# Two attentions' scores: two heads per pass on the two row halves of the array, and retention's first pair of heads moved into its value projection

## The chip, the core and the metric

The kernel runs on one core of a Trainium2 chip. TensorE (PE in the profile) multiplies matrices: it loads 128 stationary columns (a weight load, PEld in the profile), streams up to 512 moving columns past them and adds the products into PSUM. VectorE (DVE), ScalarE (ACT) and GpSimd (POOL) work element by element; SyncE (SP) issues DMAs. The metric is the device time of one execution in microseconds (us); lower is better.

## The reference, cut to what matters

The reference is a two-layer encoder trunk on x of shape (1, 512, 1024), all in float32. Each layer mixes the sequence with two mixers side by side and then runs a convolutional feed-forward part. The change touches one mixer of each layer: the dilated attention of layer 0 and the retention of layer 1.

```python
# dilated attention: 8 heads of 64; three windows, each a softmax with its own log-sum-exp
q, k = rope(q.reshape(shp)), rope(k.reshape(shp))
...
s = jnp.einsum('bdhnqe,bdhnke->bdhnqk', qb, kb) * E ** -0.5
...
# retention: 4 heads, keys of 64, values of 128, a decay per head in both directions
q = rope(q) * RET_KEY_DIM ** -0.5
k = rope(k)
...
scores = jnp.einsum('bhnid,bhnjd->bhnij', q, k) * dmat[:, None]
o = jnp.einsum('bhnij,bhnje->bhnie', scores, v)
```

The kernel computes both with the full 512 x 512 scores of a head. In dilated attention the three windows become one softmax, with the log of how many windows hold a key added to its score (the table `lnc`). In retention the chunked recurrence becomes a product of q and k, times a table of decays (`gen`), times v.

## The kernel before, in words

**Number format.** A float32 matrix is split into a high part in the format fp32r (`hi`) and the rest (`lo = x - hi`). A product a*b is then three products, hi*hi, hi*lo and lo*hi, added in PSUM (`mm3`, L262 to L265). Weights are split on arrival: ACT makes `whi`, DVE makes `wlo` (`fetch`, L240). There are four buffers each of `whi` and `wlo` (WB = 4) and three of the raw weights. `get` keeps one further weight tile ready beside the one it hands out.

**PSUM.** Two groups of four banks: `acc` (sums that live long, and the transposes `tp` of dilated attention) and `wk` (short ones; the scores `sp` of dilated attention and `rsp` of retention are here). Each bank holds 128 x 512 float32.

**Rotary and the scores.** A tile of q or k holds two heads of 64 rows each, one above the other, for all 512 positions. `rope_in` (L448) copies it out of PSUM and swaps its 32-row blocks by DMA. `rope_out` (L461) rotates it and splits it in a stacked form: one operand has, for head e, `hi` on the head's own 64 rows and `lo` on the other 64; the other operand (`moving`) has `hi` on both halves (the second by a POOL copy) and, in a second pair of columns, `lo` on the head's rows and zeros (a POOL memset) on the rest. So the three products of a head are two matrix products over all 128 rows (`mm_stack`, L483): hi*hi and lo*hi at once, then hi*lo.

**Dilated attention** (L500). After the projections of two pairs of heads and of v, a loop goes over 16 units (4 pairs of heads x 4 blocks of 128 queries). Step u issues the scores of unit u (two heads, two products each), DVE's add and minimum, ACT's exponential and POOL's scaling; the transposes (`tp`, 8 of them) of unit u-2, copied to `pT` by ACT and DVE; and the products with v (`op`) of unit u-3. Projections of the later pairs (`dqk`) stand between. In `op` the two heads lie side by side: each uses 64 of the array's 128 columns.

**Retention** (L1033). Four projections (`first`, `rqk`) give q and k; `proj_tok` (L293) makes v from four chunks of weights, 24 products each, into four banks `pt`; ACT copies them to `rv`. Then come the decay tables `gen`, the scores of head 0, and a loop over heads: the scores of head h+1, then the 16 products `ro` of head h with v. For each score tile DVE multiplies by `gen` into `sd`, which frees the `wk` bank.

**Order.** Each engine executes its own instructions strictly in the order in which they stand in its queue, and waits for others by semaphores. That order is not the one of the source: a scheduler places each instruction by its own estimate of when its operands are ready. An instruction that waits holds all that stand behind it on its engine.

Of the kernel before, what the change touches and what calls it, by code (L numbers as in the profile page):

```python
# [11 lines left out]
ALU = mybir.AluOpType  # L12
# [150 lines left out]
class K:  # L163
# [129 lines left out]
    def proj_tok(self, n, out_fn, filler=None):  # L293

        accs = [self.acc(nm=f"pt{t}") for t in range(NT)]
        for c in range(4):
            w = self.get()
            for t in range(NT):
                for j in range(2):
                    kk = 2 * c + j  # L300
                    self.mm3(accs[t], n.ht(kk, slice(t * 128, t * 128 + 128)), (w[0][:, j, :], w[1][:, j, :]), kk == 0, kk == KT - 1)
# [159 lines left out]
    def rope_out(self, pool, rope, t, sw, moving, tag, bufs):  # L461

# [37 lines left out]
    def dilated(self, n, tail):  # L500
        nc, I = self.nc, self.I
        V = nc.vector
        with ExitStack() as ctx:
# [7 lines left out]
            def project(p, what, ps=None):  # L511
# [3 lines left out]
                qk[p, what] = self.rope_out(dp, rope, *self.rope_in(dp, ps)[:2], what == "k", "d" + what, 3)  # L515
# [40 lines left out]
            for i in range(4):  # L556
# [3 lines left out]
                if i < 2:  # L560
                    qk[0, "qk"[i]] = self.rope_out(dp, rope, *rin[i][:2], i == 1, "d" + "qk"[i], 3)
            with self.tc.issue_after(rin[3][2].ins):
                for i in (2, 3):
                    qk[1, "qk"[i % 2]] = self.rope_out(dp, rope, *rin[i][:2], i == 3, "d" + "qk"[i % 2], 3)
# [468 lines left out]
    def retention(self, n, order):  # L1033
        nc, I = self.nc, self.I
        V = nc.vector
        with ExitStack() as ctx:
# [8 lines left out]
            def rot(i):  # L1045
                which, s = i // 2, i % 2
                qk[which, s] = self.rope_out(rp, rope, *rin[i][:2], which == 0, f"r{which}{s}", 1)
# [12 lines left out]
            self.proj_tok(n, lambda t, a: nc.scalar.copy(v[:, t, :], a))  # L1060
# [5 lines left out]
            for h in range(4):  # L1066
# [339 lines left out]
```

## Time and profile before

| | |
|---|---|
| time, median of 3 runs | 1319.92 us (1319.66 to 1320.06) |
| the profiled execution's own time | 1319.69 us |
| its span, first to last instruction | 1317.9 us |
| PE busy / DVE / ACT / POOL, share of the span | 99% / 57% / 40% / 11% |
| chain that ended last | PE 87%, DVE 7%, ACT 2% |
| granted TensorE clock over the span | 0.999 of full speed |

A timeline row gives an instruction's start and how long it took. On PE the second is not its cost in a stream: matrix products overlap, and the cost of one is the distance to the start of the next. A product of 512 columns takes 0.39 us from start to end, but the next one starts 0.227 us after it. Rows with xN merge N like instructions in a row; their time runs from the first start to the last end. Idle time and what ended it stand in square brackets.

### The profile page before, as it was taken

Reading aid. Unit: us, or ns where it says so; the run is one execution under the profiler, and the core shown is the slowest. Engines: PE = TensorE matmul, PEld = TensorE weight load, DVE = VectorE, ACT = ScalarE, POOL = GpSimd, SP = SyncE. Lnnn points to the kernel's source line nnn. Section 1 sums busy time; section 2 is a strip of 40 time slices with the busy share of each in tenths; the row PEclk is TensorE's granted clock in tenths of the full one; section 3 lists DMA queues with packets and bytes.
Section 4 is the critical chain, followed back from the end, with each engine's and each line's share of the span. In section 5 each row is a group of like instructions: output and inputs, shape, how many; then the busy total and the mean of one; then the engine's idle time right before and its main releaser. Section 6 shows DMA issues by size and latency. Waiting matters only on the chain.

```text
span 1317.9 us, 17629 instructions
## 1 busy us (share of the span) xinstructions
PE 1302.9 (99%) x6977; PEld 1092.6 (83%) x6977; DVE 750.7 (57%) x1089; ACT 526.9 (40%) x837; POOL 144.4 (11%) x175
## 2 busy tenths in 40 slices
PE   8999999999999999999999999999999999999997
PEld 7877888888988888888889887888888888888886
DVE  5777659977744432444437828879754443344432
ACT  5466548235433321333326334532433331133332
POOL 2454120013000000000002200024100000000001
PEclk9999999999999999999999999999999999999999
DMA  7430113411333332333323513330343333233321
GB/s 227 127 103 25 52 33 112 130 49 61 119 101 99 98 96 81 112 96 96 96 80 112 163 41 100 93 96 19 90 122 99 99 99 96 81 113 96 96 80 64
DMA packets 161025, 123.61 MB, mean 94 GB/s; under 512 B 6985, under 2 KB 134477, under 8 KB 160944
## 3 DMA queue, kind: packets, MB, share of 16 engines
q1 hardware_dynamic: 160798, 122.43, 31.6%
q8 instruction: 55, 0.90, 0.3%
q14 instruction: 26, 0.21, 0.1%
q10 hardware_dynamic: 146, 0.07, 0.0%
HBM read 117.23 MB, written 2.10 MB: 91 GB/s over the span
## 4 chain that ended last, share of the span: by engine, by line
PE 87%; DVE 7%; ACT 2%; DMA 1%; issue 1%; SPq 1%; POOL 1%; POOLq 0%; ACTq 0%; DVEq 0%
PE gup L264 11%; PE gup L265 11%; PE gup L263 11%; PE oacc L264 7%; PE oacc L265 7%; PE oacc L263 7%; PE pt L263 2%; PE pt L264 2%; PE pt L265 2%; PE first L264 2%; PE first L265 2%; PE first L263 2%; PE ap L263 1%; PE ap L264 1%; PE ap L265 1%; PE hap L263 1%
## 5 line engine op out<-in xcount | busy, mean ns | idle before, releaser
L252 DVE TENSOR_TENSOR wlo<-raw,whi 128x1024 fp32r<-128x1024 f32 x192 | 236.2, 1232 | 305.0 <-ACT whi L251 300.3
L251 ACT CAST whi<-raw 128x1024 fp32r<-128x1024 f32 (+1 forms) x197 | 206.1, 1047 | 424.7 <-PE gup L264 183.7
L263 PE MATMUL gup<-hh,whi 128*128 128x512 f32 x656 | 255.2, 389 | 0.0
L264 PE MATMUL gup<-hl,whi 128*128 128x512 f32 x656 | 255.2, 389 | 0.0
L265 PE MATMUL gup<-hh,wlo 128*128 128x512 f32 x656 | 255.2, 389 | 0.0
L263 PEld LDWEIGHTS gup<-hh,whi 128*128 128x128 f32 x656 | 123.2, 188 | 25.6
L264 PEld LDWEIGHTS gup<-hl,whi 128*128 128x128 f32 x656 | 123.2, 188 | 25.4
L265 PEld LDWEIGHTS gup<-hh,wlo 128*128 128x128 f32 x656 | 123.2, 188 | 25.4
L263 PE MATMUL oacc<-whi,ghi 128*128 128x512 f32 x352 | 137.1, 389 | 0.0
L265 PE MATMUL oacc<-whi,glo 128*128 128x512 f32 x352 | 137.0, 389 | 0.0
L264 PE MATMUL oacc<-wlo,ghi 128*128 128x512 f32 x352 | 136.9, 389 | 0.0
L265 PEld LDWEIGHTS oacc<-whi,glo 128*128 128x128 f32 x352 | 66.1, 188 | 13.7
L263 PEld LDWEIGHTS oacc<-whi,ghi 128*128 128x128 f32 x352 | 66.1, 188 | 13.7
L264 PEld LDWEIGHTS oacc<-wlo,ghi 128*128 128x128 f32 x352 | 66.1, 188 | 13.6
L428 DVE TENSOR_TENSOR sl<-gup,sl 128x512 f32<-128x512 f32 x42 | 29.0, 692 | 81.1 <-PE gup L265 81.1
L313 DVE TENSOR_TENSOR x<-oacc,x 128x512 f32<-128x512 f32 x64 | 43.2, 684 | 48.6 <-PE oacc L265 48.6
L427 ACT ACTIVATE sl<-c 128x512 f32<-128x512 f32 x44 | 27.8, 632 | 89.2 <-DVE c L365 89.2
L263 PE MATMUL first<-hh,whi 128*128 128x256 f32 x192 | 54.9, 288 | 0.0
L264 PE MATMUL first<-hl,whi 128*128 128x256 f32 x192 | 54.4, 284 | 0.2 <-DVE hl L224 0.2
L265 PE MATMUL first<-hh,wlo 128*128 128x256 f32 x192 | 54.2, 283 | 0.0
L104 POOL TENSOR_SCALAR ss<-ss 128x1 f32<-128x1 f32 x16 | 5.0, 311 | 429.3 <-ACT jk L102 429.3
L263 PE MATMUL pt<-whi,hh 128*128 128x512 f32 x128 | 50.1, 391 | 0.1
(422 smaller groups left out, 2336.4 us busy)
## 6 DMA issues: line engine op xcount, KB each, us to landing
raw<-in_ffn_w_in_dram SPq DMA_DIRECT2D x88, 512.0 KB, 3.8
raw<-in_ffn_w_out_dram SPq DMA_DIRECT2D x44, 512.0 KB, 3.7
raw<-in_ab_w_in_dram SPq DMA_DIRECT2D x28, 512.0 KB, 3.9
raw<-in_cd_w_in_dram SPq DMA_DIRECT2D x24, 512.0 KB, 4.6
x<-in_x_dram SPq DMA_DIRECT2D x16, 256.0 KB, 4.2
raw<-in_ab_w_out_dram SPq DMA_DIRECT2D x8, 512.0 KB
raw<-in_cd_w_out_dram SPq DMA_DIRECT2D x8, 512.0 KB, 3.6
rs<-rt SPq DMA_DIRECT2D x32, 64.0 KB, 2.0
```

The source lines that it names most:

```text
L104: nc.gpsimd.tensor_scalar(ss[:, 1:2], ss[:, 0:1], s, EPS, op0=ALU.add, op1=ALU.add)
L251: self.nc.scalar.copy(hi, raw)
L252: (self.nc.gpsimd if self.pool_lo else self.nc.vector).tensor_tensor(lo, raw, hi, op=ALU.subtract)
L263: mm(out, a[0], b[0], start=start, stop=False)
L264: mm(out, a[0], b[1], start=False, stop=False)
L265: return mm(out, a[1], b[0], start=False, stop=stop)
L313: self.nc.vector.tensor_add(xs, acc, xs)
L427: nc.scalar.activation(sl, c, AF.Silu)
L428: nc.vector.tensor_mul(sl, up, sl)
```

## The change

The operands of both score products are now split plainly, `hi` and `lo` of all 128 rows. The scores of the two heads of a pair are made together by `mm_pair`: six products, head 0 on rows 0 to 63 and head 1 on rows 64 to 127 of the array, three each, in turn, each head into its own PSUM bank. The POOL copies and memsets of `rope_out` go, and its ACT and DVE work is one instruction each where there were two. In retention the tables `gen` are made pair by pair inside `scores`; the scores of the first pair are issued in the value projection ahead of its chunk 3 (RS = 3), those of the second behind the products `ro` of head 0; the `sd` tiles have three buffers where there were two.

```diff
-    def proj_tok(self, n, out_fn, filler=None):
+    def proj_tok(self, n, out_fn, within={}):
...
         for c in range(4):
+            within.get(c, lambda: None)()
             w = self.get()
...
-        o = pool.tile([128, 4 if moving else 2, S], F32R, tag=tag, name=tag, bufs=bufs)
-        half = [slice(0, 64), slice(64, 128)]
-        for e in range(2):
-            a, b = half[e], half[1 - e]
-            nc.scalar.copy(o[a, e], t[a])
-            nc.vector.tensor_sub(o[a, 2 + e] if moving else o[b, e], t[a], o[a, e])
-            if moving:
-                nc.gpsimd.memset(o[b, 2 + e].bitcast(F32), 0.0)
-                nc.gpsimd.tensor_copy(o[b, e], o[a, e])
+        o = pool.tile([128, 2, S], F32R, tag=tag, name=tag, bufs=bufs)
+        self.split(o[:, 0], o[:, 1], t)
         return o
...
-    def mm_stack(self, out, a, b, e, cols):
-        self.nc.tensor.matmul(out, a[:, e, cols], b[:, e], start=True, stop=False)
-        self.nc.tensor.matmul(out, a[:, e, cols], b[:, 2 + e], start=False, stop=True)
+    def mm_pair(self, outs, a, b, cols):
+
+        for x, y in ((0, 0), (0, 1), (1, 0)):
+            for e in range(2):
+                r = slice(64 * e, 64 * e + 64)
+                self.nc.tensor.matmul(outs[e], a[r, x, cols], b[r, y], start=x + y == 0, stop=x == 1)
...
-                for e in range(2):
-                    sp = self.wk(nm="sp")
-                    self.mm_stack(sp, qk[p, "q"], qk[p, "k"], e, slice(i * 128, i * 128 + 128))
+                sps = [self.wk(nm="sp") for _ in range(2)]
+                self.mm_pair(sps, qk[p, "q"], qk[p, "k"], slice(i * 128, i * 128 + 128))
+                for e, sp in enumerate(sps):
...
-            self.proj_tok(n, lambda t, a: nc.scalar.copy(v[:, t, :], a))
...
-            def scores(h):
-                q, k = qk[0, h // 2], qk[1, h // 2]
+            def scores(s):
+                for h in (2 * s, 2 * s + 1):
+                    nc.scalar.activation(gen[:, h, :], rel[0], AF.Copy, scale=ld[:, h:h + 1])
+                    V.scalar_tensor_tensor(gen[:, h, :], rel[1], ld[:, 4 + h:5 + h], gen[:, h, :], op0=ALU.mult, op1=ALU.add)
+                    nc.scalar.activation(gen[:, h, :], gen[:, h, :], AF.Exp)
                 for j in range(4):
-                    sp = self.wk(nm="rsp")
-                    self.mm_stack(sp, k, q, h % 2, slice(j * 128, j * 128 + 128))
-                    t = rp.tile([128, S], F32, tag=f"sd{j}", name=f"sd{j}", bufs=2)
+                    sps = [self.wk(nm="rsp") for _ in range(2)]
+                    self.mm_pair(sps, qk[1, s], qk[0, s], slice(j * 128, j * 128 + 128))
...
-            scores(0)
+            self.proj_tok(n, lambda t, a: nc.scalar.copy(v[:, t, :], a), {RS: lambda: scores(0)})
...
             for h in range(4):
-                if h < 3:
-                    scores(h + 1)
...
+                if h == 0:
+                    scores(1)
...
+RS = 3
```

What this does to the order on an engine is shown at three places. PE in the last unit of dilated attention, before (`sp` are the scores, `tp` the transposes, `op` the products with v; numbers tell the banks apart):

```order
L546 MATMUL op_1233<-pT_1308,dv_196 64x128
L484 MATMUL sp_1359<-dk_1086,dq_923 128x512
L485 MATMUL sp_1359<-dk_1086,dq_923 128x512
L484 MATMUL sp_1365<-dk_1086,dq_923 128x512
L485 MATMUL sp_1365<-dk_1086,dq_923 128x512
L535 MATMUL tp_1374<-ident_76,smx_1284 128x128 x4
```

and now:

```order
L542 MATMUL op_1225<-pT_1304,dv_196 64x128
L481 MATMUL sp_1357<-dk_1078,dq_911 128x512
L481 MATMUL sp_1358<-dk_1078,dq_911 128x512
L481 MATMUL sp_1357<-dk_1078,dq_911 128x512
L481 MATMUL sp_1358<-dk_1078,dq_911 128x512
L481 MATMUL sp_1357<-dk_1078,dq_911 128x512
L481 MATMUL sp_1358<-dk_1078,dq_911 128x512
L531 MATMUL tp_1374<-ident_76,smx_1283 128x128 x4
```

The unit keeps its place between `op` and `tp`; its four products are six, and the two banks take turns.

PE at the start of the value projection's chunk 3 in retention, now (`pt` are the projection's banks, `rsp` the score tiles; before, 24 products `pt` stand here and all `rsp` come after them):

```order
L265 MATMUL pt3_6252<-whi_6285,hl1_5867 128x512
L481 MATMUL rsp_6349<-r00_6171,r10_6232 128x512
...
L481 MATMUL rsp_6362<-r00_6171,r10_6232 128x512
L263 MATMUL pt0_6249<-whi_6315,hh1_5865 128x512
L264 MATMUL pt0_6249<-wlo_6316,hh1_5865 128x512
L481 MATMUL rsp_6373<-r00_6171,r10_6232 128x512 x3
L481 MATMUL rsp_6374<-r00_6171,r10_6232 128x512 x3
L481 MATMUL rsp_6385<-r00_6171,r10_6232 128x512 x3
L481 MATMUL rsp_6386<-r00_6171,r10_6232 128x512 x3
L265 MATMUL pt0_6249<-whi_6315,hl1_5867 128x512
```

Twelve products fill the four `wk` banks, two of the projection follow, then twelve more into the same banks, here three of one head and then three of the other; the other 22 of chunk 3 stand behind them.

DVE at the same place (`r11` is the last rotated tile, `wlo` a weight tile's low part, `sd` the scores times the decays), before:

```order
L473 TENSOR_TENSOR r11_6252<-room_6223,r11_6252 64x512 x2
L252 TENSOR_TENSOR wlo_6568<-raw_6565,whi_6567 128x1024
L252 TENSOR_TENSOR wlo_6598<-raw_6595,whi_6597 128x1024
L1079 TENSOR_TENSOR sd0_6408<-rsp_6405,gen_5980 128x512
L1079 TENSOR_TENSOR sd1_6413<-rsp_6410,gen_5980 128x512
```

and now:

```order
L224 TENSOR_TENSOR r11_6238<-room_6217,r11_6238 128x512
L252 TENSOR_TENSOR wlo_6568<-raw_6565,whi_6567 128x1024
L252 TENSOR_TENSOR wlo_6598<-raw_6595,whi_6597 128x1024
L1075 TENSOR_TENSOR sd0_6357<-rsp_6349,gen_5980 128x512
L1075 TENSOR_TENSOR sd0_6359<-rsp_6350,gen_5980 128x512
```

On DVE nothing has moved: the two `wlo` still stand ahead of the first `sd`, whose scores PE now makes a chunk earlier.

DVE early in dilated attention, units 1 to 3, before (`smx<-sp` reads the scores; `dq` is the low part of the rotated q of pair 2, `pT` the copy of a transpose):

```order
L537 COPY pT<-tp 128x512
L527 RECIPROCAL st<-st 128x2
L466 TENSOR_TENSOR rt<-rt,rope 128x512
L467 TENSOR_TENSOR rt<-rt,rs 128x512
L524 ISA smx,st<-sp,lnc 128x512
...
L473 TENSOR_TENSOR dq<-rt,dq 64x512 x2
L252 TENSOR_TENSOR wlo<-raw,whi 128x1024
L527 RECIPROCAL st<-st 128x2
L537 COPY pT<-tp 128x512
```

and now:

```order
L533 COPY pT<-tp 128x512
L523 RECIPROCAL st<-st 128x2
L466 TENSOR_TENSOR rt<-rt,rope 128x512
L467 TENSOR_TENSOR rt<-rt,rs 128x512
L224 TENSOR_TENSOR dq<-rt,dq 128x512
L252 TENSOR_TENSOR wlo<-raw,whi 128x1024
L520 ISA smx,st<-sp,lnc 128x512
...
L533 COPY pT<-tp 128x512
```

Here `dq` and `wlo` have moved ahead of the two reads of unit 3's scores (`...` stands for the second one and its flag).

## Rows read from the trace of the kernel before

**Rows 1.** The page: the span, the busiest engines, and the chain of waits by engine.

```profile
span 1317.9 us, 17629 instructions
...
PE 1302.9 (99%) x6977; PEld 1092.6 (83%) x6977; DVE 750.7 (57%) x1089; ACT 526.9 (40%) x837; POOL 144.4 (11%) x175
...
PE 87%; DVE 7%; ACT 2%; DMA 1%; issue 1%; SPq 1%; POOL 1%; POOLq 0%; ACTq 0%; DVEq 0%
```

**Rows 2.** The waits of PE over the whole span, longest in total first: what waited, for whom, us in total, times, longest.

```profile
PE nrowp L91 <- DMA nrow<-in_norm_mix_dram: 3.8, 1, 3.8
PE nt L152 <- DVE xn L139: 0.8, 1, 0.8
PE tp L535 <- ACT pT L537: 0.7, 1, 0.7
```

**Rows 3.** The timeline of PE in dilated attention: one unit and the start of the next (start, time, engine, line, operation, tiles, shapes, count).

```profile
118.16 0.50 PE L484 MATMUL sp<-dk,dq 128*128 128x512 f32 x1
118.49 0.40 PE L485 MATMUL sp<-dk,dq 128*128 128x512 f32 x1
118.73 0.40 PE L484 MATMUL sp<-dk,dq 128*128 128x512 f32 x1
118.96 0.39 PE L485 MATMUL sp<-dk,dq 128*128 128x512 f32 x1
119.19 1.03 PE L535 MATMUL tp<-ident,smx 128*128 128x128 f32 x8
120.16 1.09 PE L546 MATMUL op<-pT,dv 128*64 128x128 f32 x16
121.18 0.50 PE L484 MATMUL sp<-dk,dq 128*128 128x512 f32 x1
```

**Rows 4.** The same timeline where transposes follow `op` directly, at the end of dilated attention.

```profile
130.26 1.09 PE L535 MATMUL tp<-ident,smx 128*128 128x128 f32 x8
```

**Rows 5.** The timeline of PE in the gated delta part of layer 0: transposes `vp` of 64 x 64 blocks, the first four of the x12 on rows 0 to 63, the next four on rows 64 to 127, the rest on rows 0 to 63 again, all into output rows 0 to 63; the x4 all on one half. Between them, products over the whole array.

```profile
269.35 0.63 PE L917 MATMUL vp<-ident,P 64*64 64x64 f32 x12 [0.20 <-DVE P L903]
269.92 0.50 PE L263 MATMUL oacc<-whi,yh 128*128 128x512 f32 x1
270.35 0.41 PE L917 MATMUL vp<-ident,P 64*64 64x64 f32 x4
270.69 0.50 PE L264 MATMUL oacc<-wlo,yh 128*128 128x512 f32 x1
271.02 0.39 PE L265 MATMUL oacc<-whi,yl 128*128 128x512 f32 x1
271.25 0.39 PE L263 MATMUL oacc<-whi,yh 128*128 128x512 f32 x1
```

**Rows 6.** The timeline early in dilated attention, rows of DVE, ACT and PE where PE waits.

```profile
76.33 0.69 DVE L467 TENSOR_TENSOR rt<-rt,rs 128x512 f32<-128x512 f32 x1 [1.86 <-POOL rs L465]
...
77.55 0.69 DVE L524 CUSTOM_DVE_ANT_0 smx<-sp,lnc 128x512 f32<-128x512 f32 x1
...
79.71 1.23 DVE L252 TENSOR_TENSOR wlo<-raw,whi 128x1024 fp32r<-128x1024 f32 x1
...
80.93 0.67 DVE L537 COPY pT<-tp 128x512 f32<-128x512 f32 x1
...
80.40 1.05 ACT L537 COPY pT<-tp 128x512 f32<-128x512 f32 x2
...
81.11 0.63 PE L535 MATMUL tp<-ident,smx 128*128 128x128 f32 x4 [0.70 <-ACT pT L537]
81.67 1.09 PE L546 MATMUL op<-pT,dv 128*64 128x128 f32 x16
```

**Rows 7.** The views of the tiles `dk` (the rotated, split k of dilated attention) and `gen` (retention's decays): instructions by line, time in ns, least, median and most.

```profile
L472 ACT CAST dk<-rt x4: 616/619/621, 86.7 to 115.2; 64x512 fp32r<-64x512 f32 x4
L473 DVE TENSOR_TENSOR dk<-rt,dk x4: 684/687/990, 87.4 to 115.9; 64x512 fp32r<-64x512 f32 x4
...
L1067 ACT ACTIVATE gen<-rel,ld x4: 1029/1038/1050, 710.8 to 720.4; 128x896 f32<-128x896 f32 x4
```

**Rows 8.** The timeline of PE in retention: the end of the value projection's chunk 2 and the start of chunk 3, then the products of head 1 between two heads' scores, and the first product after retention.

```profile
743.03 0.39 PE L265 MATMUL pt<-whi,hl 128*128 128x512 f32 x1
743.26 0.39 PE L263 MATMUL pt<-whi,hh 128*128 128x512 f32 x1
...
757.76 3.73 PE L1089 MATMUL ro<-rv,sd 128*128 128x128 f32 x32
761.25 0.47 PE L484 MATMUL rsp<-r,r 128*128 128x512 f32 x1
761.56 0.39 PE L485 MATMUL rsp<-r,r 128*128 128x512 f32 x1
...
770.24 0.47 PE L263 MATMUL pt<-whi,hh 128*128 128x512 f32 x1
```

**Rows 9.** The timeline of ACT and DVE in retention, around the weights `whi` and `wlo` that stand ahead of the first `sd`.

```profile
709.73 1.08 ACT L223 CAST hh<-nt 128x512 fp32r<-128x512 f32 x2 [2.51 <-PE nt L152]
...
743.69 2.00 ACT L251 CAST whi<-raw 128x1024 fp32r<-128x1024 f32 x2
...
744.77 2.36 DVE L252 TENSOR_TENSOR wlo<-raw,whi 128x1024 fp32r<-128x1024 f32 x2 [0.32 <-ACT whi L251]
749.35 4.87 DVE L1079 TENSOR_TENSOR sd<-rsp,gen 128x512 f32<-128x512 f32 x8 [2.22 <-PE rsp L485]
```

More of the change, by code (lines that the diff above doesn't have):

```diff
@@ L459, in rope_in, with rope_out @@
         return t, sw, ins
-    def rope_out(self, pool, rope, t, sw, moving, tag, bufs):
+    def rope_out(self, pool, rope, t, sw, tag, bufs):
         nc = self.nc
@@ L514, in project @@
                     self.proj_t(self.get(), n, ps)
-                qk[p, what] = self.rope_out(dp, rope, *self.rope_in(dp, ps)[:2], what == "k", "d" + what, 3)
+                qk[p, what] = self.rope_out(dp, rope, *self.rope_in(dp, ps)[:2], "d" + what, 3)
             def scores(p, i):
@@ L560, in dilated @@
                 if i < 2:
-                    qk[0, "qk"[i]] = self.rope_out(dp, rope, *rin[i][:2], i == 1, "d" + "qk"[i], 3)
+                    qk[0, "qk"[i]] = self.rope_out(dp, rope, *rin[i][:2], "d" + "qk"[i], 3)
             with self.tc.issue_after(rin[3][2].ins):
                 for i in (2, 3):
-                    qk[1, "qk"[i % 2]] = self.rope_out(dp, rope, *rin[i][:2], i == 3, "d" + "qk"[i % 2], 3)
+                    qk[1, "qk"[i % 2]] = self.rope_out(dp, rope, *rin[i][:2], "d" + "qk"[i % 2], 3)
             self.proj_tok(n, lambda t, a: nc.scalar.copy(v[:, t, :], a))
@@ L1046, in rot @@
                 which, s = i // 2, i % 2
-                qk[which, s] = self.rope_out(rp, rope, *rin[i][:2], which == 0, f"r{which}{s}", 1)
+                qk[which, s] = self.rope_out(rp, rope, *rin[i][:2], f"r{which}{s}", 1)
             for i in range(4):
@@ L1065, in retention @@
             nc.sync.dma_start(ld, bc(I["ret_log_decay"].rearrange("o d h -> o (d h)"), [128, 8]))
-            for h in range(4):
-                nc.scalar.activation(gen[:, h, :], rel[0], AF.Copy, scale=ld[:, h:h + 1])
-                V.scalar_tensor_tensor(gen[:, h, :], rel[1], ld[:, 4 + h:5 + h], gen[:, h, :], op0=ALU.mult, op1=ALU.add)
-                nc.scalar.activation(gen[:, h, :], gen[:, h, :], AF.Exp)
             sd = {}
-            def scores(h):
-                q, k = qk[0, h // 2], qk[1, h // 2]
+            def scores(s):
[3 more added lines that the diff above has]
+                    nc.scalar.activation(gen[:, h, :], gen[:, h, :], AF.Exp)
                 for j in range(4):
-                    sp = self.wk(nm="rsp")
-                    self.mm_stack(sp, k, q, h % 2, slice(j * 128, j * 128 + 128))
-                    t = rp.tile([128, S], F32, tag=f"sd{j}", name=f"sd{j}", bufs=2)
+                    sps = [self.wk(nm="rsp") for _ in range(2)]
+                    self.mm_pair(sps, qk[1, s], qk[0, s], slice(j * 128, j * 128 + 128))
                     o = 384 - 128 * j
-                    V.tensor_mul(t, sp, gen[:, h, o:o + 512])
-                    sd[h, j] = t
-            scores(0)
+                    for e, sp in enumerate(sps):
+                        h = 2 * s + e
+                        t = rp.tile([128, S], F32, tag=f"sd{j}", name=f"sd{j}", bufs=3)
+                        V.tensor_mul(t, sp, gen[:, h, o:o + 512])
+                        sd[h, j] = t
+            self.proj_tok(n, lambda t, a: nc.scalar.copy(v[:, t, :], a), {RS: lambda: scores(0)})
             O = [self.acc((128, 4, 128), f"ro{t}") for t in range(4)]
             for h in range(4):
-                if h < 3:
-                    scores(h + 1)
                 for i in range(4):
@@ L1089, in retention @@
                         nc.tensor.matmul(O[i][:, h, :], sd[h, j][:, i * 128:(i + 1) * 128], v[:, j, h * 128:(h + 1) * 128], start=(j == 0), stop=(j == 3))
+                if h == 0:
+                    scores(1)
             Os = []
             for t in range(4):
-                o = rp.tile([128, 4, 128], F32, tag=f"sd{t}", name=f"ros{t}", bufs=2)
+                o = rp.tile([128, 4, 128], F32, tag=f"sd{t}", name=f"ros{t}", bufs=3)
                 (V.tensor_copy if t % 2 else nc.scalar.copy)(o, O[t])
```

## The prediction

> **What bounds the kernel now.** I read the page first: PE is busy for 99% of the span and holds 87% of the chain that ended last [rows 1]. Then the waits of PE: after the start (3.8 us for a DMA, 0.8 us for the first transposes) one wait of 0.7 us in dilated attention is the longest [rows 2]. So between about 25 us and the end PE runs almost without a stop, and what the change does to the time is what it does to PE's queue. What DVE, ACT and POOL save counts only where PE waits for them. Then the timelines of the two parts. In dilated attention a unit takes 121.18 - 118.16 = 3.02 us [rows 3]: four score products, eight transposes, sixteen `op`. In the stream a 512-column product starts 0.227 us after the one before (743.03 to 743.26 [rows 8]).
>
> **The products.** Per pair of heads and block of 128 rows, four products over 128 rows become six over 64. There are 16 such units in dilated attention and 8 in retention. What six cost depends on whether the two halves run side by side. The nearest rows are the `vp` transposes: four of one kind take 0.41 us, twelve take 0.63 us [rows 5], so eight more add 0.22 us, 0.028 each. Four alone, with 0.245 us for the last from start to end, step by (0.41 - 0.245)/3 = 0.055. The first eight are four on rows 0 to 63 and four on rows 64 to 127 with the same output rows: they ran in pairs. `op`, two heads on two column halves, agrees: sixteen start within about 1.0 us where eight transposes of the same 128 columns, over the whole array, take 0.97 (119.19 to 120.16 [rows 3]). So I take a pair at the price of one product: three steps of 0.227 for six. The upper bound is no overlap, six steps.
> The products then save 16 x 0.227 = 3.63 us in dilated attention and 8 x 0.227 = 1.82 us in retention.
>
> **The switches.** Rows 3 to 5 show what a change between the whole array and part of it costs. From the last of eight transposes (0.109 apart, so at 119.19 + 0.76 = 119.95) to the first `op` pass 0.21 us instead of 0.11; from `op` to `sp`, the first score product starts late and the second 0.33 us behind it (118.16 to 118.49) instead of 0.227. Eight transposes behind `op` last 1.09 us [rows 4], behind scores 1.03 [rows 3]; with their late start of 0.09 that is 0.15 us. After `vp`, the whole-array product starts 0.09 late and the next one follows after 0.33 [rows 5]. So: 0.2 us into a stretch of 512-column products, 0.15 us into transposes.
> The Trainium skill says the same as a rule, and it speaks against this change ("TensorEngine Tiling (Array Packing)", section "Tiling Modes"): a change of the tiling mode, not of the tile alone, drains the engine. The rows agree for 128 x 64 and 64 x 64 tiles; none shows 64 x 128, the mode of the new scores.
> Before, scores ran in the same mode as the transposes behind them; only `op` to `sp` paid. Now every stretch of scores pays at its end, and also at its start where no `op` precedes. By the new order there are 15 stretches in dilated attention: 14 end at transposes (14 x 0.15 = 2.1), one at a projection (0.2); six begin behind a projection (6 x 0.2 = 1.2), the other nine behind `op`, which paid before too. Sum 3.5 us, against the 3.63 saved: dilated attention gains 0.13 us. Bounds: no switch cost for this mode gives -3.63; if the two weight loads of a first pair go one after the other, the second waits another 0.11 (as much as the first `op`-to-`sp` excess), 15 times: +1.5.
> A sentence of the skill on that load, apart from the sum: "TensorE: Matmul & The Clock Gate", section "LDWEIGHTS", lets a load of 128 columns take as long for few rows as for 128, an estimate of 0.107 us; two in a row fit into a step of 0.227, so a pair would stay at the price of one product. No row here has such a pair.
>
> **Dilated attention's one wait.** PE stood 0.70 us before 81.11 for ACT's `pT` [rows 6]. On ACT the copy of unit 1's transposes now stands ahead of unit 3's exponentials, which helps. But DVE now does `dq` and `wlo` before unit 3's two score reads, and its own `pT` comes behind them. Worked through: `rt` ends at 77.02; ACT's split takes 0.62 and DVE's 0.69 after it [rows 7], to 78.3; ACT's `whi`, 1.05, follows its split and ends at 78.7; `wlo` 1.23 ends at 79.9; two reads at 0.61 each end at 81.1; `pT` starts at 81.15 instead of 80.93, and `op` (81.67) moves by the same 0.2 to 0.3 us. I take +0.2. Bounds: the wait vanishes, -0.95 (with its neighbour's delay); another weight tile falls in, +1.2.
>
> **Retention, first pair.** Chunk 2 ends and the scores begin at 743.26 instead of a projection product. DVE's `sd` comes behind two `wlo`. The second of them needs a `whi` buffer that chunk 2 has just left (four buffers; chunk 3 and two later tiles hold the others), so its `whi` cannot start before about 743.45, however early the rotary work is done. Then 1.05 for `whi` to 744.5, 1.22 for `wlo` to 745.75, 0.69 for the first `sd`: 746.45, and PE may go on at 746.55 [rows 8, 9]. PE is there at 743.26 + 0.2 + 6 x 0.227 + 0.2 + 2 x 0.227 + 0.1 = 745.6: it waits about 1 us. From there each triple of products needs one more `sd`, at 4.87/8 = 0.61 us: the last triple starts at 746.55 + 3 x 0.61 = 748.4, ends at 749.06, and with 0.2 us for the switch the projection goes on at 749.26. That is 6.0 us, 0.45 of them the two projection products; before, the 16 products cost 3.63. So +1.9 us.
> **Second pair.** 24 products in a row into four banks. The switch 0.2, three steps 0.68, 0.2 until DVE can read: `sd` from 1.1; the fourth bank comes free at 1.1 + 3 x 0.61 + 0.69 + 0.1 = 3.7, the last six products end at 4.4, the switch back 0.1: 4.5 us. Before: 3.63 and twice 0.09 for entering from `ro` (761.25 to 761.56, 0.31 against 0.227 [rows 8]) = 3.8. So +0.7 us. Behind it nothing waits: head 1's `sd` are old.
> The bounds of both together: -1.82 + 1.2 (three stretches at 0.4) = -0.6 if DVE holds nothing up, and +4 if one more `wlo` of 1.2 us falls among the `sd`.
>
> **At nothing.** POOL's copies and memsets, and half of ACT's and DVE's splits, go: PE does not wait there in retention, whose q and k are due only at 743. On ACT two `gen` (1.04 each [rows 7]) now stand ahead of the last two `hh`: ACT was idle for 2.51 us before them [rows 9], and that holds the two; if the small table `ld` has not landed by then, `hh` is late and PE with it, up to 1 us. SP issues `ld` one weight tile earlier, nothing else moves there. The third `sd` buffers cost no time.
>
> **The sum.** -0.13 + 0.2 + 1.9 + 0.7 = +2.7 us on the profiled 1319.69 (span 1317.9 and 1.8 around it), 1322.4 us. That execution stands 0.2 us below the median of 1319.92, so against the median it is +2.5 us, +0.19%. A measurement of this kernel can tell about 0.2% from no change: 2.64 us, to 1322.56.
>
> **The rivals.**
> 1. *No drain for the row mode.* For: another tile shape than any in the rows. Against: three shapes in rows 3 to 5 all pay. The 3.5 us of dilated attention go, and some 0.5 in retention, whose ends DVE sets: 1322.4 - 4.0 = 1318.4.
> 2. *The halves don't run side by side* (slower). PE takes the six one after the other. For: no row has 512 columns in fp32r on row halves. Against: `vp`. Dilated attention: 16 x 2 x 0.227 + 3.5 = +10.8; first pair: PE reaches the second twelve at 747.0, ends at 749.9, +2.6; second: 0.35 + 24 x 0.227 = 5.8, +2.0; with 0.2 above +15.6: 1335. Between the cases, each 0.01 us that a pair costs above 0.227 adds 72 x 0.01 = 0.7 us.
> 3. *PE's gaps close* (faster). No drain, `wlo` out of the way of `sd`, and the 0.95 us wait gone: dilated -3.63 - 0.95; first pair 1.3 us sooner (`sd` from 744.4), +0.6; second without switches, +0.4: -3.6, 1316. For: ACT and DVE have less to do. Against: the order of DVE's queue and the `whi` buffer.
>
> **Chances.** The forecast with its own range of 1320.6 to 1324.6 has 0.58, and the bound of 1322.56 cuts it in half: 0.29 no change, 0.29 slower. Rival 1 has 0.17 (no change), rival 2 0.09 (slower), rival 3 0.16 (faster). So faster 0.16, no change 0.46, slower 0.38. The range leaves out rival 2 and half of rival 3: 1317.0 to 1325.6.
>
> **What would show it.** Right: `sp` in pairs that start a few ns apart, six within about 0.8 us; 0.1 us lost into the transposes behind; a unit of about 2.93 us; `rsp` waiting for DVE's `sd` by about 1 us in the first pair and again between blocks of the second; `wlo` directly ahead of the first `sd`. Wrong: single `sp` 0.227 apart; transposes following without loss; `sd` starting at 744.5; or PE waiting elsewhere, as on `hh` near 712.

## The result and the profile after

The changed kernel takes 1326.34 us (median; 1326.06 to 1329.17) beside 1319.79 us for the kernel before on the same chip: ratio 1.0052, 95% interval 1.0042 to 1.0063. It is slower by 6.6 us. The forecast was 1322.4 us, with a range up to 1325.6, so the time lies outside the range. The sign had the chance of 0.38.

The page of after: PE is as full as in [rows 1], with 3.6 us more of busy time; DVE, ACT and POOL have lost 10, 7 and 18 us, which bought nothing.

```profile
span 1324.5 us, 17672 instructions
...
PE 1306.5 (99%) x7025; PEld 1088.4 (82%) x7025; DVE 740.8 (56%) x1077; ACT 519.5 (39%) x825; POOL 126.6 (10%) x151
```

The waits of PE in after (us in total, times, longest). The wait of `tp` for ACT [rows 2] is gone; in its place `op` waits twice for DVE's `pT`, and `rsp`, `hm` and `first` are new or longer.

```profile
PE op L542 <- DVE pT L533: 1.4, 2, 1.0
PE rsp L481 <- DVE sd L1075: 0.8, 1, 0.8
PE hm L1144 <- DMA w<-in_hy_w_dram: 0.8, 1, 0.8
...
PE first L264 <- DVE hl L224: 0.7, 1, 0.7
```

To see where the time went, take the start of the same group of products in both timelines, and follow by how much after is late. The steps between two such places are what a stage lost:

| place | before | after | late by | lost since the row above |
|---|---|---|---|---|
| first projection of layer 0 | 25.67 | 25.89 | 0.22 | 0.22 |
| last `op` of dilated attention | 133.33 | 135.25 | 1.92 | 1.70 |
| second half of `first` in retention | 709.88 | 711.85 | 1.96 | 0.04 |
| `rqk` (behind the late `hh`, `hl`) | 721.47 | 724.33 | 2.86 | 0.90 |
| first projection behind the heads' outputs | 770.24 [rows 8] | 776.03 | 5.79 | 2.93 |
| hyena's first filter product `hm` (PE's last product is 6.58 late) | 803.88 | 810.35 | 6.47 | 0.68 |

The timeline of PE in dilated attention, one unit (as [rows 3]):

```profile
117.02 0.97 PE L481 MATMUL sp<-dk,dq 64*128 64x512 f32 x6
117.92 1.09 PE L531 MATMUL tp<-ident,smx 128*128 128x128 f32 x8
118.94 1.09 PE L542 MATMUL op<-pT,dv 128*64 128x128 f32 x16
119.97 0.97 PE L481 MATMUL sp<-dk,dq 64*128 64x512 f32 x6
```

Six products on row halves take 0.90 us up to the transposes, and a unit 119.97 - 117.02 = 2.95 us (3.02 before, 2.93 forecast). The transposes behind scores last 1.09 instead of 1.03: that is the change of shape.

The first wait, near 81 us (timelines of DVE and PE in after):

```profile
78.34 0.69 DVE L224 TENSOR_TENSOR dq<-rt,dq 128x512 fp32r<-128x512 f32 x1 [0.68 <-ACT dq L223]
79.29 1.23 DVE L252 TENSOR_TENSOR wlo<-raw,whi 128x1024 fp32r<-128x1024 f32 x1 [0.26 <-ACT whi L251]
80.43 0.68 DVE L520 CUSTOM_DVE_ANT_0 smx<-sp,lnc 128x512 f32<-128x512 f32 x1
...
81.65 0.68 DVE L533 COPY pT<-tp 128x512 f32<-128x512 f32 x1
...
80.93 0.43 PE L542 MATMUL op<-pT,dv 128*64 128x128 f32 x2
82.39 1.09 PE L542 MATMUL op<-pT,dv 128*64 128x128 f32 x14 [1.03 <-DVE pT L533]
```

DVE does `dq`, `wlo` and two score reads, and only then the `pT` for which PE stands. The second wait has the same form; here it is the rotary product `rt`, 1.55 us long, that stands ahead of `pT`:

```profile
98.41 1.55 DVE L466 TENSOR_TENSOR rt<-rt,rope 128x512 f32<-128x512 f32 x1
99.88 0.68 DVE L533 COPY pT<-tp 128x512 f32<-128x512 f32 x1
...
99.82 0.43 PE L542 MATMUL op<-pT,dv 128*64 128x128 f32 x2
100.61 1.09 PE L542 MATMUL op<-pT,dv 128*64 128x128 f32 x14 [0.35 <-DVE pT L533]
```

Retention in after (timelines of ACT, DVE and PE; the row at 747.80 is two products of the projection between the two twelves):

```profile
711.77 1.98 ACT L1065 ACTIVATE gen<-rel,ld 128x896 f32<-128x896 f32 x2 [2.65 <-DMA ld<-in_ret_log_decay_dram]
713.66 1.05 ACT L223 CAST hh<-nt 128x512 fp32r<-128x512 f32 x2
...
747.45 1.23 DVE L252 TENSOR_TENSOR wlo<-raw,whi 128x1024 fp32r<-128x1024 f32 x1 [3.48 <-ACT whi L251]
748.59 4.87 DVE L1075 TENSOR_TENSOR sd<-rsp,gen 128x512 f32<-128x512 f32 x8
...
745.89 0.39 PE L265 MATMUL pt<-whi,hl 128*128 128x512 f32 x1
746.21 1.66 PE L481 MATMUL rsp<-r,r 64*128 64x512 f32 x12
747.80 0.50 PE L263 MATMUL pt<-whi,hh 128*128 128x512 f32 x1
...
749.33 2.75 PE L481 MATMUL rsp<-r,r 64*128 64x512 f32 x12 [0.79 <-DVE sd L1075]
752.01 0.51 PE L265 MATMUL pt<-whi,hl 128*128 128x512 f32 x1
...
757.15 3.78 PE L1083 MATMUL ro<-rv,sd 128*128 128x128 f32 x32
760.86 4.50 PE L481 MATMUL rsp<-r,r 64*128 64x512 f32 x24
765.29 10.98 PE L1083 MATMUL ro<-rv,sd 128*128 128x128 f32 x96
776.03 0.48 PE L263 MATMUL pt<-whi,hh 128*128 128x512 f32 x1
```

ACT stands 2.65 us for the table `ld`, and the last two `hh` stand behind it: 3.9 us later than in [rows 9], of which 2.0 is the lag up to there. The first twelve products take 746.21 to 747.80, 1.59 us; the next twelve 752.01 - 749.33 = 2.68, at DVE's pace of 0.61 a read.

### The profile page after: what moved, and what is told of

It is laid out like the page before. It is cut to its first block, busy times and chain, and to the rows that moved or that the text cites. A ratio compares the mean times of both kernels' runs of the same rounds, so it can differ in the third digit from the quotient of the medians.

```text
span 1324.5 us, 17672 instructions
## 1 busy us (share of the span) xinstructions
PE 1306.5 (99%) x7025; PEld 1088.4 (82%) x7025; DVE 740.8 (56%) x1077; ACT 519.5 (39%) x825; POOL 126.6 (10%) x151
## 4 chain that ended last, share of the span: by engine, by line
PE 86%; DVE 8%; ACT 2%; issue 2%; DMA 1%; POOL 1%; SPq 0%; POOLq 0%; ACTq 0%; DVEq 0%
PE gup L263 11%; PE gup L265 11%; PE gup L264 11%; PE oacc L265 7%; PE oacc L264 7%; PE oacc L263 7%; PE first L264 2%; PE pt L265 2%; PE first L263 2%; PE pt L263 2%; PE pt L264 2%; PE first L265 2%; PE ap L264 1%; PE ap L263 1%; PE ap L265 1%
## 5 line engine op out<-in xcount | busy, mean ns | idle before, releaser
L265 PE MATMUL pt<-whi,hl 128*128 128x512 f32 x128 | 50.0, 390 | 0.0
```

What stands on the lines that cost most here:

```text
L265: return mm(out, a[1], b[0], start=False, stop=stop)
```

## The experiments

Theory A, after reading the two traces: the loss is the sum of local waits for DVE and ACT, whose queues the new order has rearranged, with retention's pairs as forecast; the products and the changes of shape alone are about even. The rivals: the parts disturb each other; the changes of shape cost more than they seem; the pairs are cheap only by the way they are issued. Times are medians, ratios are to the kernel before on the same chip, with the 95% interval.

**1. Each part alone.** `dilated_alone` has retention, its scores and its rotary splits as before; `retention_alone` the same for dilated attention.

```diff
-                    sps = [self.wk(nm="rsp") for _ in range(2)]
-                    self.mm_pair(sps, qk[1, s], qk[0, s], slice(j * 128, j * 128 + 128))
+                    sp = self.wk(nm="rsp")
+                    self.mm_stack(sp, k, q, h % 2, slice(j * 128, j * 128 + 128))
```

> Dilated attention as changed, retention as before. Theory A (the loss is the sum of local waits seen in the trace of after): dilated attention alone costs +1.6 us, of which two waits of PE's op for DVE's pT (near 82 and 100 us) are some 1.3; nothing else changes: 1319.8 + 1.6 = 1321.4. Theory B (the two waits belong to that one execution, the rest of the part is even): 1319.8 to 1320.3.

> Retention as changed, dilated attention as before. Theory A: late hh and hl +0.9, the scores' 48 products +2.9, and +0.6 before hyena's first filter product if that wait is caused by retention: 1323.6 without, 1324.2 with it. Theory B (the two parts disturb each other): the two losses alone add up to clearly less than 6.5, so under 1323.0 here.

Measured: 1322.53 us, 1.0020 (1.0011 to 1.0028), and 1323.51 us, 1.0026 (1.0017 to 1.0035). The two excesses over 1320.07 add up to 2.46 + 3.44 = 5.9 of the 6.55. The missing 0.6 lies inside the intervals, so there is no sign that the parts disturb each other. `dilated_alone` is 1.1 us above its expectation. Its trace has dilated attention at +1.8 (late by 1.04 at 25.67 and by 2.85 at 133.33), and the same two waits of 1.4 us; the rest is at the start and in front of `hm`, where it waits 1.2 us though hyena and retention are those of before (see "Elsewhere" below).

**2. `gen` behind the last `hh`** (`gen_held`).

```diff
-                    nc.scalar.activation(gen[:, h, :], rel[0], AF.Copy, scale=ld[:, h:h + 1])
+                    with self.tc.issue_after(n.last.ins):
+                        nc.scalar.activation(gen[:, h, :], rel[0], AF.Copy, scale=ld[:, h:h + 1])
```

> After, with ACT's gen held behind the last hh. Theory A (ACT stands 2.65 us for the table ld with hh queued behind it): PE's wait of 0.9 us near 715 goes, 1326.3 - 0.9 = 1325.4. Theory B (the late hh is covered later, or the held gen is late for something else): 1326.0 to 1326.5.

Measured: 1325.00 us, 1.0039 (1.0027 to 1.0052). `hh` runs at 711.70 and `gen` at 712.66; PE's wait for `hl` is gone, and the product at 776.03 comes at 775.14, 0.9 us sooner. Theory A holds.

**3. A head's three products together** (`heads_apart`).

```diff
-        for x, y in ((0, 0), (0, 1), (1, 0)):
-            for e in range(2):
+        for e in range(2):
+            for x, y in ((0, 0), (0, 1), (1, 0)):
```

> After, with the three products of one head issued together and then those of the other, in place of in turn. Theory A (a pair costs one product only because the halves run side by side, and they do so only in turn): 3 more steps of 0.227 in each of 16 units, 10.9 us in dilated attention; in retention 12 more steps in each pair of heads, 5.4 us, less some 2 us in which PE waited for DVE: 1326.3 + 14 = 1340. Theory B (the halves overlap in any order, or not at all): 1326 to 1327.

Measured: 1324.78 us, 1.0036 (1.0023 to 1.0048). Both expectations were wrong: theory A by 15 us, and it is faster than after instead of level with it. PE's queue has three products of one head and then three of the other, and yet six take what they took in turn; and the edit moved DVE's `pT` ahead of the rotary product near 98 us (timelines of PE and DVE):

```profile
115.86 0.97 PE L481 MATMUL sp<-dk,dq 64*128 64x512 f32 x6
...
97.72 0.69 DVE L533 COPY pT<-tp 128x512 f32<-128x512 f32 x1
98.33 1.49 DVE L466 TENSOR_TENSOR rt<-rt,rope 128x512 f32<-128x512 f32 x1
```

The second wait is gone (the first is now 0.6, for ACT's `pT`), and dilated attention loses 0.77 instead of 1.70. So the same products with the same changes of shape cost 0.9 us less when DVE's queue stands in another order.

**4. The three `wlo` that fall into dilated attention, on POOL.** `wlo_pool` missed: it put on POOL the tiles fetched in dilated attention's own code. The `wlo` at 79.29 is the delta net's, brought forward by the schedule, and stayed on DVE. `next3_pool` moves that one and the two after it.

```diff
-            (self.nc.gpsimd if self.pool_lo else self.nc.vector).tensor_tensor(lo, raw, hi, op=ALU.subtract)
+            self.pool_left -= 1
+            (self.nc.gpsimd if self.pool_lo or 0 <= self.pool_left else self.nc.vector).tensor_tensor(lo, raw, hi, op=ALU.subtract)
...
+            self.pool_left = 3
             return self.by_tile(self.y_list(yh, yl))
```

> After, with the wlo of the weight tiles that are fetched in dilated attention on POOL instead of DVE. Theory A (PE's two waits for pT are DVE's queue: wlo of 1.23 us ahead of the score reads near 79 us, the rotary product of 1.55 ahead of pT near 98): DVE has five wlo less, the waits of 1.0 and 0.35 (with what they drag along, 1.3) shrink by 1 or more: 1325.3 or less. Theory B (POOL at work slows DVE down, or POOL's wlo of 2.4 us comes late): 1326.0 or more.

> After, with the three wlo that the delta net's weights bring into dilated attention on POOL. Theory A (DVE's queue): PE's wait of 1.0 us for pT near 82 us goes, op there comes 1.0 us earlier against the start of that stretch, and dilated attention costs at most 0.9 us instead of 1.7: about 1325.4. Theory B (the changes of shape cost it, and another wait takes over): dilated attention stays at 1.5 or more.

Measured: `wlo_pool` 1325.43 us, 1.0045 (1.0031 to 1.0058), between the two theories, with both waits as in after, so it tells nothing of them. The 0.9 us that it gains on after lie elsewhere: the late `hh` cost it 0.32 instead of 0.90 us, and `hm` waited 0.4 instead of 0.8. `next3_pool` 1325.25 us, 1.0041 (1.0029 to 1.0054). Its PE near 81 us, and POOL's `wlo`:

```profile
80.90 1.09 PE L544 MATMUL op<-pT,dv 128*64 128x128 f32 x16
81.93 0.96 PE L483 MATMUL sp<-dk,dq 64*128 64x512 f32 x6
...
79.31 2.38 POOL L254 TENSOR_TENSOR wlo<-raw,whi 128x1024 fp32r<-128x1024 f32 x1 [2.40 <-ACT whi L252]
```

The sixteen `op` run through; sp comes at 81.93 instead of 83.41. Dilated attention goes from 0.13 us late to 0.28: it loses 0.15 us. So of the 1.70 us about 1.5 go when DVE no longer has those three `wlo`. The edit also makes the schedule anew, so the figure is for load and order on DVE together. Not all of it shows in the time, since in the profiled execution `ld` landed 7.2 us after its issue (6.05 in after) and the late `hh` and `hl` cost PE 2.0 us instead of 0.90.

**5. Where the first pair stands** (`pair_behind`).

```diff
-            self.proj_tok(n, lambda t, a: nc.scalar.copy(v[:, t, :], a), {RS: lambda: scores(0)})
+            self.proj_tok(n, lambda t, a: nc.scalar.copy(v[:, t, :], a))
+            scores(0)
```

> After, with retention's first pair of scores behind the value projection again. Theory A (DVE's eight sd of 0.61 us bind a pair wherever it stands, and the first heads' outputs wait for seven of them): 0.1 + 0.7 + 0.2 + 7 x 0.61 + 0.7 = 6.0 us against 5.4 inside the projection, 1326.3 + 0.5 = 1326.8. Theory B (inside, the pair is held up by wlo, and behind the projection it is not): 1325.0 to 1325.8.

Measured: 1325.87 us, 1.0043 (1.0030 to 1.0057). From the first `rsp` to the end of head 0's outputs it takes 760.12 - 751.24 = 8.88 us; less 3.49 for 32 `ro` [rows 8] that is 5.4, as inside the projection (752.01 - 746.12 - 0.45 = 5.44). The total lies between the two theories and bears out neither. By the trace the pair itself costs the same at either place, and the stage loses (775.28 - 770.24) - (723.92 - 721.47) = 2.59 us where after loses 2.93. Most of the 0.5 us by which the total is under after is not the pair's: `ld` landed 5.6 us after its issue here, and the late `hh` cost 0.49 us instead of 0.90.

**6. Two blocks a stretch** (`spread`, with the edit of `gen_held`).

```diff
-                if h == 0:
-                    scores(1)
+                    if (h, i) in ((0, 3), (1, 1)):
+                        blocks(1, (2 * h, 2 * h + 1))
...
-            self.proj_tok(n, lambda t, a: nc.scalar.copy(v[:, t, :], a), {RS: lambda: scores(0)})
+            gens(0)
+            gens(1)
+            self.proj_tok(n, lambda t, a: nc.scalar.copy(v[:, t, :], a), {2: lambda: blocks(0, (0, 1)), 3: lambda: blocks(0, (2, 3))})
```

> gen_held, with retention's scores in four stretches of two blocks (12 products, four banks): two inside the value projection, one behind head 0's outputs, one within head 1's. Theory A (PE waits for DVE only because more blocks stand in a row than there are banks; a stretch costs 1.59 us from first to last start and 0.2 for the two changes): 4 x 1.79 = 7.2 us against 9.9 now, and no wait at the end of head 0: 1325.0 - 3.0 = 1322.0. Theory B (the changes of tile shape are what retention pays for, and there are as many again): 1325 or more.

Measured: 1322.11 us, 1.0017 (1.0008 to 1.0026). Theory A holds. PE waits for no `sd` (timeline):

```profile
758.02 1.66 PE L482 MATMUL rsp<-r,r 64*128 64x512 f32 x12
759.61 2.05 PE L1089 MATMUL ro<-rv,sd 128*128 128x128 f32 x16
761.59 1.67 PE L482 MATMUL rsp<-r,r 64*128 64x512 f32 x12
763.19 9.20 PE L1089 MATMUL ro<-rv,sd 128*128 128x128 f32 x80
```

Retention goes from 2.03 us late to 1.90: it loses nothing.

**7. That retention with dilated attention as before** (`retention_spread`, the edits of `retention_alone` and `spread`).

> Dilated attention as before, retention as in spread (with gen held). Theory A (retention lost 2.9 us to waits for DVE, and 0.9 to the late hh): with neither it is level with the kernel before, 1319.8 (0.1 saved). Theory B (the six changes of shape cost more than the steps that the pairs save): 1321 or more.

Measured: 1319.87 us, 1.0001 (0.9992 to 1.0010). Level with the kernel before, as theory A had it. Four reads of DVE behind a stretch in place of eight, with `gen` held behind `hh`, make good all of retention's loss. There is no gain either: by the figures above, a stretch of twelve costs 1.59 us and about 0.2 for the two changes of shape (0.32 and 0.34 us between starts there, instead of 0.227), beside 8 x 0.227 = 1.82 for the eight products that it replaces. The 0.2 is an estimate; the trace has retention 1.17 us late before and 1.09 behind.

**8. Dilated attention in twos.** `twos` takes two units at a time: 12 `sp`, 16 `tp`, 32 `op`. `twos_spread` adds the edits of `spread`.

```diff
-            for u in range(len(units) + 3):
+            for b in range(0, len(units) + 4, 2):
+                two = units[b:b + 2]
+                sps = [products(*x) for x in two]
+                for x, y in zip(two, sps):
+                    scores(*x, y)
...
-                    tp = TPD(self)((128, 4, 128), "tp")
+                    tp = (self.wk if i % 2 else self.acc)((128, 4, 128), "tp")
```

> After, with the units of dilated attention in twos: 12 products, 16 transposes, 32 op in a row in place of 6, 8, 16. Theory A (a unit loses 0.58 us to three changes of tile shape: 2.95 less 3 x 0.227, 8 x 0.109 and 8 x 0.102): half of that, 16 x 0.29 = 4.6 us, goes: 1326.3 - 4.6 = 1321.7, less up to 1.3 if the two waits for pT go as well. Theory B (DVE and ACT, with twice the products to read at once, hold PE up as much): 1326 or more.

> The edits of gen_held, spread and twos together. Theory A (all three losses are local and add up): 1326.3 - 1.3 - 3.0 - 4.6 = 1317.4, faster than the kernel before by 2.5 us. Theory B (they come back as waits elsewhere): 1320 or more.

Measured: 1326.17 us, 1.0046 (1.0033 to 1.0058), and 1321.85 us, 1.0016 (1.0007 to 1.0024): theory B in both. The trace of `twos` has both mechanisms (timeline of PE):

```profile
81.71 1.24 PE L534 MATMUL tp<-ident,smx 128*128 128x128 f32 x8 [1.58 <-DVE st L523]
...
126.01 1.65 PE L481 MATMUL sp<-dk,dq 64*128 64x512 f32 x12
...
131.38 1.97 PE L534 MATMUL tp<-ident,smx 128*128 128x128 f32 x16
```

Two units without a wait take 131.38 - 126.01 = 5.37 us, 0.27 less per unit than 2.95; the 0.29 of theory A are there. But five waits for DVE's reciprocals, 4.0 us in all, take it back: they stand behind `wlo` and four score reads.

**9. More versions of that.** In all of them DVE's or the banks' wait came back elsewhere. `twos_pvfirst` puts `op` ahead of `tp`; `twos_later` turns units two later; `twos_pool` and `twos_next3` are `twos_spread` with the `wlo` of `wlo_pool` and of `next3_pool` on POOL. Of `twos_later`:

```diff
-                if b >= 2:
-                    for x in units[b - 2:b]:
+                if b >= 4:
+                    for x in units[b - 4:b - 4 + 2]:
                         turn(*x)
```

> twos_spread, with op of the units before ahead of the transposes instead of behind them. Theory A (twos saved 4 us of changes and lost 4 us to transposes that waited for DVE's reciprocals; with 2 us of op ahead of them these waits go): 1321.9 - 4 = 1317.9, up to 1.5 more if the next scores wait for the banks of the last transposes. Theory B (DVE has too much to do, and the wait only changes its place): 1321 or more.

> twos_pvfirst, with the transposes another two units later (12 buffers for the exponentials, 4 instead of 8 for pT). Theory A: the reciprocals are 5 us old when their transposes come, no wait is left before tp, 1317.5; at most 0.5 below twos_pvfirst. Theory B (the wait has gone to the scores, for banks or buffers): no better than twos_pvfirst.

> twos_spread with the same wlo on POOL. Theory A (its five waits of tp for the reciprocals, 3.5 us, stand behind wlo and score reads on DVE): the longest shrink by 1.2 each, 1321.9 - 2.5 = 1319.4, level with the kernel before or faster by 0.5. Theory B: 1321.5 or more.

> twos_spread with the same three on POOL. Theory A: the waits of tp behind wlo and score reads (1.6, 0.3, 1.7, 0.2 and 0.25) shrink where a wlo of 1.2 stood ahead (near 80 and 92 us): 1321.9 - 1.5 = 1320.4. Theory B (DVE's four score reads in a row are enough to hold the transposes up): 1321.5 or more.

Measured: 1325.71 us, 1.0041 (1.0029 to 1.0054), with the waits now before `sp`, for the banks of the last transposes (1.7 us) and for `dk` (0.9), and PE's clock down for some 10 us (below); 1322.14 us, 1.0019 (1.0010 to 1.0028), one wait of 2.3 for reciprocals and 1.8 us of waits before `sp`; 1323.57 us, 1.0026 (1.0017 to 1.0036), five waits of 4.1 us together (3.5 in `twos_spread`); 1321.31 us, 1.0013 (1.0004 to 1.0021), two waits left, of 2.7 us together. Theory B is borne out by `twos_pvfirst` and `twos_pool`. `twos_later` fits neither: it misses theory A by 4.6 us, but it is 3.6 us faster than `twos_pvfirst`, where B had no gain; most of that may be what the half clock cost `twos_pvfirst`. `twos_next3` lies between the two, 0.2 us under B's bound and 0.9 above A's value.

**10. The best of the single units.** `spread_apart` is `spread` with the order of `heads_apart`; the other two put the `wlo` of 4 on POOL.

> spread, with the three products of a head issued together as in heads_apart; every product is the same, and DVE's queue in dilated attention gets the order of heads_apart (pT ahead of the rotary product near 98 us). Theory A (dilated attention's loss is mostly DVE's queue order: +1.7 us with the order of after, +0.8 with that one): 1322.1 - 0.9 = 1321.2. Theory B (the gain of heads_apart was another's): 1322.0 or more.

> spread_apart with the same wlo on POOL. Theory A: its two waits before tp in dilated attention (0.6 and 0.3 us) go: 1321.7 - 0.8 = 1320.9, a unit's gain of 0.07 and the changes beside projections left. Theory B as for wlo_pool: 1321.7 or more.

> spread_apart with the same three on POOL. Theory A: its wait of 0.6 us before tp near 81 us goes: 1321.7 - 0.6 = 1321.1; dilated attention then costs some 0.3 us more than before. Theory B: 1321.7 or more.

Measured: 1321.68 us, 1.0014 (1.0005 to 1.0023); 1321.17 us, 1.0010 (1.0001 to 1.0019); 1321.64 us, 1.0013 (1.0004 to 1.0022). The first lies between the theories, and its trace sides with A: dilated attention loses 0.90 (0.22 to 1.12) where `spread` loses 1.7. The second too lies between the theories; in it the two waits stayed, as in `wlo_pool`. The third is at theory B's bound: in it a wait of 1.3 us for POOL's `wlo` replaced that of 0.6: POOL takes 2.4 us for it and `smx` queues behind. No version beat the kernel before.

## Why the prediction was wrong

The terms of the sum, in the order in which they stand on record:

- **A pair at the price of one product:** right. Six in 0.97 us from first start to last end, 2.95 us a unit where 2.93 was forecast. Rival 2 falls.
- **The switches:** right. Rival 1 falls, as scores and the transposes behind them pay in every unit. Without the waits, dilated attention's balance is +0.46 us (1.70 less 0.46 and 0.78 for the two waits, each read as the lateness gained across it), 0.40 of it in `tp` and `op` behind the last scores; forecast were -0.13. From the second wait to the last scores the lateness falls from 1.59 to 1.46, which is that -0.13. The 0.40 is again DVE's queue (timelines below): the new order has `yl`, which waits 0.31 us for ACT, ahead of both reads of the last unit's scores, where before one read came first. So POOL's last `smx` starts at 133.25, and the last `tp` at 134.00 instead of right behind the `op` of 132.80. This is read from the traces; no run tested it.

After:

```profile
130.03 0.69 DVE L224 TENSOR_TENSOR yl<-op,yh 128x512 fp32r<-128x512 f32 x1 [0.31 <-ACT yh L223]
130.64 0.68 DVE L520 CUSTOM_DVE_ANT_0 smx<-sp,lnc 128x512 f32<-128x512 f32 x1
...
133.25 1.36 POOL L525 TENSOR_SCALAR smx<-smx,st 128x512 f32<-128x512 f32 x2 [2.00 <-DVE st L523]
...
134.00 1.32 PE L531 MATMUL tp<-ident,smx 128*128 128x128 f32 x8
```

Before:

```profile
128.12 0.69 DVE L524 CUSTOM_DVE_ANT_0 smx<-sp,lnc 128x512 f32<-128x512 f32 x1
...
128.73 0.69 DVE L224 TENSOR_TENSOR yl<-op,yh 128x512 fp32r<-128x512 f32 x1
```

- **"Dilated attention's one wait":** this is the step that failed. +0.2 us stood on record; the two waits cost 0.46 + 0.78 = 1.2. For the first, the order was as told (`dq`, `wlo`, two reads, `pT`), and the times were 0.5 us too early: `pT` began at 81.65, not at 81.15, because `rt` ended at 77.65, not at 77.02. Ahead of `rt`'s partner `rs` on POOL stood a scaling `smx` that waited 0.98 us for DVE's reciprocal, which the working had not looked at; PE was itself 0.3 to 0.4 us late by then, so only part of the 0.5 adds to its wait:

```profile
73.88 1.79 POOL L525 TENSOR_SCALAR smx<-smx,st 128x512 f32<-128x512 f32 x2 [0.98 <-DVE st L523]
```

The second wait was not looked for. The trace of before shows no wait there, and I worked through only the one that it does show; but the new order had moved `rt` ahead of `pT` there too, where before `pT` came first. With DVE's three `wlo` elsewhere the stage loses 0.15 (`next3_pool`).
- **Retention, first pair:** right. `sd` was to start 2.49 us after the scores' place in the queue and started 748.59 - 746.12 = 2.47 after it. PE's wait of "about 1 us" is 0.79; the cost is 5.44 - 3.63 = 1.81, forecast 1.9. `wlo` stands directly ahead of the first `sd`.
- **Second pair:** right. 765.29 - 760.86 = 4.43, forecast 4.5. The whole stage lost 2.93 where 2.6 stood: the pairs cost 1.81 + 0.62 = 2.4, and 0.5 is in the `ro` products, which the sum had at nothing (3.71 us for head 0 behind the projection and 10.74 for three heads, 14.45 in all, against 13.95 before).
- **"At nothing", `gen` ahead of `hh`:** the second failure. The condition was named (`ld` not landed) with its price, up to 1 us; it was put at nothing, and cost 0.90. `ld` was issued a weight tile earlier but landed 6.05 us after its issue; `gen` waited for it with `hh` behind. The sign named for it, PE waiting on `hh`, is in the trace, and `gen_held` shows that this alone is worth 0.9.
- **Elsewhere:** 0.2 at the start and 0.6 to 0.7 before hyena's `hm`, where nothing was changed. Among the traces here the wait before `hm` is 0 to 1.3 us and the lag at the first projection 0.06 to 1.15. The lag may be a matter of the single execution: it is largest, 1.15, in `retention_spread`, whose median is level with before. The wait before `hm` seems to go in part with the program. `hm` needs loads that SP issues before and behind four small tables `bf` (`w` before, `mlp` behind). In the three traces with dilated attention as before (before, `retention_alone`, `retention_spread`) each of these issues takes 0.6 us; in all seventeen with it changed one of them takes 0.99 to 1.61, and `mlp` is issued that much later. In after, then before:

```profile
802.43 1.07 SPq L1140 DMA_DIRECT2D bf<-in_hy_f_dram  x1
...
796.53 0.60 SPq L1144 DMA_DIRECT2D bf<-in_hy_f_dram  x1
```

The lengths don't follow each other closely (`gen_held` has an issue of 1.00 us and a wait of 0.16), so the cause stays open, and so does how much of the 0.9 the medians carry.

One reading in the prediction was off without a consequence: of the four products `vp`, 0.245 us is the length of the first, and the last takes 0.216; the steps between them, on which the price of a pair rests, are as told.

So of the 6.5 us in the profile 3.2 were forecast in kind and about in size (retention 2.93, the even products, 0.2 of the waits), 1.0 is the unseen part of dilated attention's waits, 0.9 the late table, 0.4 the end of dilated attention, and the remaining 0.9 lies where the change is not, at the start and before `hm`. Rival 3, that PE's gaps close, needed a queue that DVE did not have: in `next3_pool` the gap of before is gone, in the changed kernel it is not.

"TensorEngine Tiling (Array Packing)" in the Trainium skill, section "Performance Considerations", warns of a part of what decided here: tiling speeds TensorE, not the reading of its banks, which can become the bottleneck. The trace agrees in retention: twelve products take 1.59 us, and DVE needs 8 x 0.61 = 4.87 us for the eight results of 24.

## What to carry to other kernels

A kernel in which one engine is 99% busy, as here, can lose time by the order of the other engines' queues although those engines have time to spare. This change only saved work there, and yet it reordered them, and such a new order must be walked through at every place where the full engine reads from them, not only where the old trace shows a wait. When products get cheaper, count the reads that follow them: more results in a row than there are banks put the full engine at the reader's pace, as with the second twelve in retention; two stretches of half the length cost two more changes and here saved 3 us. A small table behind large loads should not stand ahead of anything that the full engine needs.

## What the runs showed of the hardware that was not expected

The two row halves keep step even when one head's three products are issued before the other's. In `heads_apart` six take 0.97 us as in after, so a half need not wait until products for the other half have run. The starts show it: they come in pairs, at 115.86 and 115.87, 116.20 and 116.21, and 116.44 twice, one of each head. The Trainium skill says as much: in "TensorEngine Tiling (Array Packing)", section "Tiling Modes", tiles load weights and multiply in parallel. What stands ahead of the prediction, that an engine executes its instructions strictly in the order of its queue, does not hold in this trace across the two row halves of PE. The forecast of 1340 had taken the queue to be strictly in turn.

In `twos_pvfirst` the granted clock fell to half (1.2 of 2.4 GHz). The stretches (us, then busy time of PE, PEld, DVE, ACT and POOL, the granted clock, DMA share and rate):

```profile
94.00:97.00 3.00, 1.43 (x7) 0.64 (x6) 1.85 (x6) 3.00 (x9) 2.29 (x4) 0.98 0.71 185
97.00:100.00 3.00, 2.85 (x15) 2.10 (x16) 2.43 (x5) 0.71 (x2) 2.61 (x2) 0.50 0.06 17
100.00:104.00 4.00, 4.00 (x26) 2.92 (x23) 2.95 (x10) 3.08 (x8) 0.75 (x2) 0.50 0.00 0
104.00:108.00 4.00, 4.00 (x22) 3.62 (x20) 1.00 (x3) 1.17 (x2) 1.15 (x2) 0.61 0.02 4
```

PE had stood still for 1.66 us just before, and then ran for some 10 us at half speed. Half of that stretch, about 5 us, is an estimate of the loss; the kernel is 3.6 us slower than `twos_later` and 3.9 slower than `twos_spread`. In `twos_pool` (from 103.0) and `twos_next3` (from 100.1) the clock was at half too, each time for 3.4 us, right behind waits of 1.67 and 2.08 us. Waits of 1.58 and 1.67 us in `twos` and of 2.29 us in `twos_later` left it at 1.00. So the clock fell next to a wait in the three kernels where it fell, but the length of the wait does not tell when; no run shows that the wait was the cause.
